# Differential attention: one VectorE operation combines the two maps of a tile, where VectorE, ScalarE and GpSimd shared it

## The chip, the cores and the metric

One core of one Trainium2 chip runs the whole program once. Its engines work side by side, each on its own list of instructions in a fixed order: TensorE (PE, with its weight loads shown apart as PEld), VectorE (DVE), ScalarE (ACT), GpSimd (POOL), and SyncE (SP), which issues most transfers. They wait for each other by semaphores. The metric is the device time of the program in microseconds (us), the median of several runs; less is better.

## What is computed

The reference is one step of a two-layer network over 1280 tokens (1024 sample tokens, 256 prompt tokens). The part that matters here is the differential attention of layer 0: eight heads, each with two attention maps, whose softmaxes are subtracted before they meet the values:

```python
s = jnp.einsum('bqhmd,bkhmd->bhmqk', qi, kf) * (DH ** -0.5)   # m = 0, 1: two maps
p = jax.nn.softmax(s, axis=-1)
a = p[:, :, 0] - lam * p[:, :, 1]
return jnp.einsum('bhqk,bkhe->bqhe', a, vf)
```

A block of 128 queries sees 1280 keys (sample queries: 1024 sample keys and 256 cached ones) or 256 keys (prompt queries). The factor `lam` is one number.

## The kernel before

`stage_b` does the attention of all eight heads. A head has ten query tiles of 128 queries, `qt` 0 to 9; tiles 0 to 7 are sample tiles with 1280 keys, tiles 8 and 9 prompt tiles with 256. So there are 64 wide tiles and 16 narrow ones. Each engine's order is the order in which the Python loop over `(h, qt)` calls the steps (`manual_schedule`); there is no planner. One round of that loop works on three tiles at once: `t`, whose scores are new, `u`, the tile before, and `p`, the tile two before (`LAG`).

The steps of a wide tile `t`:

- `scores` (L987, L988): TensorE writes the two maps' scores to PSUM, `X0` and `X1` (1024 keys each) and `Y` (the other 256 keys of both).
- `maxima` (L1003, L1005, L1007): VectorE takes the maxima, from PSUM, and joins them in a 128x1 operation `mx` (L1007) whose two inputs are both in SBUF.
- `exps` (L1013, L1014): ScalarE writes the exponentials to SBUF, `e0` and `e1` (128x1280 each, f32), with their sums. `e0` has three buffers, `e1` two.
- `ratio` (L1020 to L1025): VectorE makes `r`, per query: minus `lam` times the sum of map 0 over the sum of map 1.
- `combine` (L1031, L1033, L1034): `e0 + r * e1`, written into `e0`. The first 256 columns are one VectorE operation (L1031), called right behind `ratio`. The other 1024 are a ScalarE multiplication (L1033) and a GpSimd addition (L1034), called at the end of the round.
- `turn` (L1043, L1046, L1047): TensorE transposes `e0` in three groups (four, four and two blocks of 128) into one of two PSUM buffers `tp`; ScalarE writes the rounded part `ath`, VectorE the rest `atl`, and that subtraction frees the buffer. The groups of four come one round after the tile's scores, the group of two another round later.
- `values` (L46 to L48, `pv`): TensorE multiplies pairs of tiles with the values.

Between these steps the loop puts pieces of two projections (`fill`, L46 to L48, `acc`), the last steps of the head before (`finish`: `sq` on GpSimd L1063, `zb` on VectorE L1074, and others; `ms`, L1067, are 20 one-column products of it on TensorE), and the splitting of the next weights into a rounded part on ScalarE (L41) and a remainder on GpSimd (`wlo`, L42). At the end of a head's tile 9 (8 in the last head) stands a product for the modulation, `mp` (L84), whose result VectorE adds (L85).

Of the kernel before, what the change touches and what calls it, by code (L numbers as in the profile page):

```python
# [14 lines left out]
OP = mybir.AluOpType  # L15
# [350 lines left out]
class Weights:  # L366
# [5 lines left out]
    def next(s, key, steps=False):  # L372

        if s.gen is None:
            s.start()
        while s.step():
            pass
        w, s.gen = s.ahead, None
        assert s.rest.pop(0)[0] == key
        if s.rest and s.rest[0][1] is not None:  # L380
            s.start()
            while not steps and s.step():
                pass
        return w
# [520 lines left out]
def stage_b(c, wp):  # L905


    nc, tc, a, o = c.nc, c.tc, c.a, c.o
    c.dYb = c.dram.tile([128, HB, NT], F32, name="dYb")
    c.dYa = c.dram.tile([128, HB, NT], F32, name="dYa")  # L910
    with ExitStack() as es:
# [7 lines left out]
        v = nc.vector  # L919
        values_of, late = {}, []  # L920

        def flush():
            while late:
                late.pop(0)()

        def gate_steps(hd):
            hd.zb = ev.tile([128, NT], F32, name="zb", bufs=2)
            yield from z_steps(c, pa, hd.zb, 32 + hd.h, hd.h < HB - 1, late)

        def value_steps(h):  # L930

            x = ev.tile([128, NT], F32, name="x", tag="x")
            yield from project_steps(c, pa, c.w.next(('in', 32 + h), True), c.hhi, c.hlo,
                                     lambda p, off, n: nc.scalar.copy(x[:, off:off + n], p), late=late)
            flush()
            nc.sync.dma_start(o['new_cache_v'][h], x[:, LS:NT])
            vh = kq.tile([128, 12, 128], F32R, name="vh", bufs=2)
            vl = kq.tile([128, 12, 128], F32R, name="vl", bufs=2)
            values_of[h] = vh, vl
            raw_dma(nc, vh[:, 10:12], c.dVc[0][:, h])  # L940
            raw_dma(nc, vl[:, 10:12], c.dVc[1][:, h])
            n = 8 if h else 4
            for i in range(0, 10, n):
                w = min(n, 10 - i)
                p = (ps.tile([128, 8, 128], F32, name="vt", tag=f"X{i // 8}") if h else
                     pt.tile([128, 4, 128], F32, name="vt", tag="tp"))
                for q in range(w):
                    nc.tensor.transpose(p[:, q], x[:, (i + q) * 128:(i + q + 1) * 128], c.ident)
                nc.scalar.copy(vh[:, i:i + w], p[:, :w])
                v.tensor_sub(vl[:, i:i + w], p[:, :w], vh[:, i:i + w].bitcast(F32))  # L950
            yield

        def new_head(h):
            hd = Ctx()
            hd.h = h
            hd.s = sm.tile([128, 2, 10], F32, name="s", bufs=3)
            hd.kx = [kx.tile([128, 1280], F32R, name=f"kx{m}") for m in range(2)]
            for m in range(2):
                raw_dma(nc, hd.kx[m][:, 0:LS], c.dK[m][h][:, 0:LS])
                raw_dma(nc, hd.kx[m][:, LS:1280], c.dKc[m][:, h])  # L960
            return hd

        def prompt_keys(hd):
            hd.kp = [kq.tile([128, 256], F32R, name=f"kp{m}") for m in range(2)]
            for m in range(2):
                raw_dma(nc, hd.kp[m], c.dK[m][hd.h][:, LS:NT])

        def load_queries(h, qt):
            q = []
            for n, d in (("qh", c.dQh), ("ql", c.dQl)):  # L970
                t = kx.tile([128, 2, 128], F32R, name=n, bufs=2)
                src = d[h].rearrange("(m e) q -> e m q", m=2)[:, :, qt * 128:(qt + 1) * 128]
                for r in range(2):
                    raw_dma(nc, t[r * 64:(r + 1) * 64], src)
                q.append(t)
            return q
# [47 lines left out]
            v.reciprocal(t.r, sc[:, 1:2])  # L1024
            v.scalar_tensor_tensor(t.r, t.r, sc[:, 0:1], c.nlam, op0=OP.mult, op1=OP.mult)  # L1025

        def combine(t, half):

            e, nk = t.e, HALF if t.qt < 8 else 256
            if half == 0:  # L1030
                v.scalar_tensor_tensor(e[0][:, :nk], e[1][:, :nk], t.r, e[0][:, :nk], op0=OP.mult, op1=OP.add)  # L1031
            elif t.qt < 8:
                nc.scalar.mul(e[1][:, nk:], e[1][:, nk:], t.r)  # L1033
                nc.gpsimd.tensor_add(e[0][:, nk:], e[0][:, nk:], e[1][:, nk:])  # L1034

        def turn(t, b):

# [11 lines left out]
        def values(t):  # L1049
            qp, hd = t.qt // 2, t.hd  # L1050
            v0, v1 = values_of[hd.h]
            kts = [0, 1, 2, 3, 4, 5, 6, 7, 10, 11] if qp < 4 else [8, 9]
            pv = pa.tile([128, 256], F32, name="pv", tag="acc")
            for i, kt in enumerate(kts):
                mm3(nc, pv, v0[:, kt], v1[:, kt], t.at[:, i], t.al[:, i], i == 0, i == len(kts) - 1)
            nc.scalar.copy(hd.O[:, qp * 256:(qp + 1) * 256], pv)  # L1056
# [33 lines left out]
        with tc.manual_schedule(engines={ET.PE, ET.DVE, ET.Activation, ET.Pool}):  # L1090
            fill, fin, last = [value_steps(0)], [], None
            units = [(h, qt) for h in range(HB) for qt in range(10)]
            heads = {0: new_head(0)}
            tiles = {}

            def steps(q, n):
                while n and q:
                    if next(q[0], True):
                        q.pop(0)
                    else:  # L1100
                        n -= 1

            def new_tile(i):
                t = tiles[i] = Ctx()
                h, t.qt = units[i]
                t.hd, t.q = heads[h], load_queries(h, t.qt)

            new_tile(0)
            for i in range(len(units) + LAG):
                qt = i % 10  # L1110
                t, u, p = tiles.get(i), tiles.get(i - 1), tiles.pop(i - LAG, None)
                if t:
                    hd = t.hd
                    if qt == 0:
                        prompt_keys(hd)
                    if i + 1 < len(units):
                        new_tile(i + 1)
                    if qt == 8 and hd.h < HB - 1:
                        heads[hd.h + 1] = new_head(hd.h + 1)
                    if qt == 4:  # L1120
                        fill.append(value_steps(hd.h + 1) if hd.h + 1 < HB else gate_steps(hd))
                    if qt == 9 and hd.h + 1 < HB:
                        fill.append(gate_steps(hd))
                if t:
                    scores(t)
                if p and p.qt == 9:
                    values(p)
                    steps(fin, 1)
                if t:
                    maxima(t, 0)  # L1130
                steps(fill, PRE.get(qt, 0))
                lo = turn(p, 8) if p else lambda: None
                if t:
                    exps(t, 0)
                lo()
                if t:
                    maxima(t, 1)
                    exps(t, 1)
                steps(fin, FIN.get(qt, 0))
                c.w.step()  # L1140
                if p and p.qt % 2:
                    if p.qt < 9:
                        values(p)
                    if p.qt == 7:
                        fin.append(finish(p.hd))
                        steps(fin, 1)
                if t:
                    ratio(t)
                    combine(t, 0)
                steps(fill, FILL[qt] if i > 2 else 2)  # L1150
                if t and qt == (9 if hd.h + 1 < HB else 8):
                    c.mod[0].product(*mw, ps.tile([2, 128], F32, name="mp", tag="X1"))
                if u:
                    if u.qt == 0:
                        u.hd.O = wk.tile([128, NT], F32, name="O")
                    if u.qt % 2 == 0:
                        last = [wk.tile([128, 10, 256], F32R, name=n) for n in ("ath", "atl")]
                    u.at, u.al = last
                    turn(u, 0)()
                    turn(u, 4)()  # L1160
                flush()
                if t:
                    combine(t, 1)
                    if qt == 2:
                        mw = ev.tile([128, KC, 128], F32, name="mw", tag="zb" if hd.h + 1 < HB else "x", bufs=2 if hd.h + 1 < HB else 1)
                        mw = c.mod[0].load(16 + hd.h, mw, mwb)
            steps(fin, 100)
# [3 lines left out]
FILL = (2, 1, 0, 0, 2, 0, 2, 0, 0, 2)  # L1171
PRE = {8: 1, 9: 1}
LAG = 2
HALF = 256


def rope_tables():
# [844 lines left out]
```

## Time and profile before

| | |
|---|---|
| median of 3 runs | 2818.1 us (2816.56 to 2818.32) |
| the profiled execution | 2815.8 us, span 2814.0 us |
| granted TensorE clock, mean over the span | 0.962 |
| busy share of the span | PE 92%, PEld 80%, DVE 64%, ACT 38%, POOL 18% |
| stage with the attention | about 798 to 1500 us of the span |

The span is what the trace covers; the execution's time has 1.8 us more around it. Busy shares are averages over the whole span, and stages differ. A matmul's time in the trace overlaps that of the next one, so the share of PE says little of how much more it could do. In a row of the timeline the time of an operation overlaps that of the next by about 0.08 us on DVE and ACT, so the step from start to start is what counts there. A waiting operation on DVE that has been started shows as a longer operation, not as idle time.

### The profile page before, as it was taken

What the parts mean: (1) busy time and instruction counts of PE and PEld (TensorE: products, weight loads), DVE (VectorE), ACT (ScalarE), POOL (GpSimd) and SP (SyncE); (2) the same over time, 40 slices, a digit from 0 to 9 for tenths busy, and PEclk for the clock granted to TensorE, in tenths of its full rate; (3) what the DMA queues carried; (4) which work ended last, traced back from release to release, by engine and by line L of the source; (5) the groups of instructions that cost most, each with busy time, mean ns of one, the idle gap of its engine ahead of it and who ended that gap; (6) DMA issues with size and microseconds to landing.
All of it is one profiled execution on the core that took longest, in us unless ns stands there. A gap on an engine that the chain in (4) does not pass through costs nothing.

```text
span 2814.0 us, 40016 instructions
## 1 busy us (share of the span) xinstructions
PE 2578.0 (92%) x14905; PEld 2252.4 (80%) x14905; DVE 1812.6 (64%) x3636; ACT 1073.0 (38%) x2136; POOL 512.2 (18%) x434
## 2 busy tenths in 40 slices
PE   8989889995589999999998999978999999999998
PEld 6777777774577888878777878868999989999786
DVE  6889998997456787777876866675234435664332
ACT  3342233211156676666754221563223333222311
POOL 0000000000013232232331000005123333332321
PEclk9999999997899999999998999989999999999999
DMA  5534575455732221222217973322221136654422
GB/s 223 179 116 110 165 213 190 170 198 153 193 83 80 80 87 50 86 87 83 87 49 177 311 261 116 116 72 96 97 90 69 51 110 236 195 162 155 145 80 93
DMA packets 249130, 374.01 MB, mean 133 GB/s; under 512 B 39492, under 2 KB 172134, under 8 KB 245350
## 3 DMA queue, kind: packets, MB, share of 16 engines
q1 hardware_dynamic: 217160, 320.27, 36.0%
q10 hardware_dynamic: 31632, 50.53, 6.0%
q8 instruction: 117, 1.92, 0.3%
q14 instruction: 77, 0.63, 0.1%
q0 software_dynamic: 144, 0.66, 0.1%
HBM read 254.06 MB, written 104.73 MB: 128 GB/s over the span
## 4 chain that ended last, share of the span: by engine, by line
PE 46%; DVE 11%; ACT 5%; DMA 3%; issue 2%; POOL 1%; SPq 0%; DVEq 0%; ACTq 0%; POOLq 0%
PE pf L47 6%; PE pf L46 6%; PE pf L48 6%; PE oa L46 4%; PE oa L48 4%; PE oa L47 4%; ACT e L1013 2%; DVE mx L1003 2%; PE acc L46 2%; PE acc L48 2%; PE acc L47 2%; DVE atl L1047 2%; DMA owf<-w_out_o 1%; DVE e L1031 1%; ACT e L1014 1%
## 5 line engine op out<-in xcount | busy, mean ns | idle before, releaser
L48 PE MATMUL acc<-hhi,wlo 128*128 128x512 f32 (+1 forms) x1152 | 415.1, 362 | 30.3 <-DVE wlo L42 30.2
L46 PE MATMUL acc<-hhi,whi 128*128 128x512 f32 (+1 forms) x1152 | 418.7, 363 | 11.0 <-ACT O L1056 6.5
L47 PE MATMUL acc<-hlo,whi 128*128 128x512 f32 (+1 forms) x1152 | 415.3, 361 | 0.9 <-DVE hlo L218 0.2
L1034 POOL TENSOR_TENSOR e<-e,e 128x1024 f32<-128x1024 f32 x64 | 152.4, 2382 | 1106.8 <-DMA vh<-dVc 802.4
L48 PEld LDWEIGHTS acc<-hhi,wlo 128*128 128x128 f32 x1152 | 221.1, 192 | 67.8 <-DVE wlo L42 37.5
L46 PE MATMUL oa<-owh,oyh 128*128 128x512 f32 x640 | 254.1, 397 | 6.9 <-DVE t L1372 4.4
L46 PEld LDWEIGHTS acc<-hhi,whi 128*128 128x128 f32 x1152 | 221.1, 192 | 46.9 <-ACT O L1056 11.0
L48 PE MATMUL oa<-owh,oyl 128*128 128x512 f32 x640 | 253.2, 397 | 1.7 <-POOL oyl L42 1.7
L47 PE MATMUL oa<-owl,oyh 128*128 128x512 f32 x640 | 253.7, 396 | 0.0
L47 PEld LDWEIGHTS acc<-hlo,whi 128*128 128x128 f32 x1152 | 221.1, 192 | 34.6 <-DVE hlo L218 4.6
L1013 ACT ACTIVATE e<-X,mx 128x1024 f32<-128x1024 f32 x128 | 142.8, 1116 | 122.0 <-DVE mx L1007 118.8
L41 ACT CAST whi<-wf 128x512 fp32r<-128x512 f32 x146 | 89.7, 620 | 208.7 <-DMA wf<-w_glu 45.2
L1003 DVE TENSOR_REDUCE mx<-X 128x1 f32<-128x1024 f32 x128 | 155.2, 1212 | 18.9 <-PE X L988 18.9
L42 POOL TENSOR_TENSOR wlo<-wf,whi 128x512 fp32r<-128x512 f32 x64 | 83.7, 1308 | 416.1 <-ACT whi L41 400.5
L42 DVE TENSOR_TENSOR wlo<-fold,whi 128x512 fp32r<-128x512 f32 x94 | 84.4, 911 | 107.2 <-ACT whi L41 106.2
L46 PEld LDWEIGHTS oa<-owh,oyh 128*128 128x128 f32 x640 | 121.0, 189 | 37.2 <-ACT oyh L41 3.5
L48 PEld LDWEIGHTS oa<-owh,oyl 128*128 128x128 f32 x640 | 121.2, 189 | 30.7 <-POOL oyl L42 2.6
L47 PEld LDWEIGHTS oa<-owl,oyh 128*128 128x128 f32 x640 | 121.2, 189 | 27.8
L1046 ACT CAST ath<-atp 128x512 fp32r<-128x512 f32 (+1 forms) x208 | 99.3, 513 | 102.0 <-PE atp L1043 100.5
L46 PE MATMUL pf<-heh,whi 128*128 128x322 f32 x400 | 126.5, 320 | 10.7 <-ACT heh L1542 9.0
L1043 PE MATMUL atp<-ident,e 128*128 128x128 f32 x672 | 107.2, 287 | 21.7 <-DVE atl L1047 14.3
L47 PE MATMUL pf<-hel,whi 128*128 128x322 f32 x400 | 126.0, 315 | 0.4 <-DVE hel L1543 0.3
(448 smaller groups left out, 6745.6 us busy)
## 6 DMA issues: line engine op xcount, KB each, us to landing
wf<-w_in_e SPq DMA_DIRECT2D x96, 256.0 KB
raw<-w_fno SPq DMA_DIRECT2D x16, 1024.0 KB
mw<-w_mod SPq DMA_DIRECT2D x24, 512.0 KB
stg<-w_modT SPq DMA_DIRECT2D x24, 512.0 KB
u<-dU SPq DMA_DIRECT2D x16, 640.0 KB
dz<-z SPq DMA_DIRECT2D x8, 1280.0 KB
zc<-dz SPq DMA_DIRECT2D x16, 640.0 KB
qh<-dQh SPq DMA_DIRECT2D x160, 64.0 KB
```

The costliest lines, as they stand in the source:

```text
L41: nc.scalar.copy(hi, src)
L42: (le or nc.gpsimd).tensor_sub(lo, src, hi.bitcast(F32))
L46: nc.tensor.matmul(out, whi, xhi, start=start, stop=False)
L47: nc.tensor.matmul(out, whi, xlo, start=False, stop=False)
L48: nc.tensor.matmul(out, wlo, xhi, start=False, stop=stop)
L1003: v.tensor_reduce(t.mx[:, 0, m:m + 1], t.X[m], axis=AX.X, op=OP.max, negate=True)
L1013: nc.scalar.activation(t.e[m][:, :LS], t.X[m], AF.Exp, bias=b, accum_out=t.sums[:, 0, m:m + 1])
L1014: nc.scalar.activation(t.e[m][:, y0:y0 + 256], t.Y[:, m], AF.Exp, bias=b, accum_out=t.sums[:, 1, m:m + 1])
L1034: nc.gpsimd.tensor_add(e[0][:, nk:], e[0][:, nk:], e[1][:, nk:])
L1043: nc.tensor.transpose(p[:, i], t.e[0][:, (b + i) * 128:(b + i + 1) * 128], c.ident)
L1046: nc.scalar.copy(hi, p[:, :w])
L1047: return lambda: v.tensor_sub(t.al[:, b:b + w, o], p[:, :w], hi.bitcast(F32))
```

## The change

`combine` has no halves any more: where the 256-column VectorE operation stood it is now one VectorE operation over all 1280 columns of a wide tile. The ScalarE multiplication and the GpSimd addition, and the second call at the end of the round, are gone. Narrow tiles are as before. The arithmetic is the same: `e0 + r * e1`.

```diff
-        def combine(t, half):
-
-            e, nk = t.e, HALF if t.qt < 8 else 256
-            if half == 0:
-                v.scalar_tensor_tensor(e[0][:, :nk], e[1][:, :nk], t.r, e[0][:, :nk], op0=OP.mult, op1=OP.add)
-            elif t.qt < 8:
-                nc.scalar.mul(e[1][:, nk:], e[1][:, nk:], t.r)
-                nc.gpsimd.tensor_add(e[0][:, nk:], e[0][:, nk:], e[1][:, nk:])
+        def combine(t):
+
+            e, nk = t.e, 1280 if t.qt < 8 else 256
+            v.scalar_tensor_tensor(e[0][:, :nk], e[1][:, :nk], t.r, e[0][:, :nk], op0=OP.mult, op1=OP.add)
...
                 if t:
                     ratio(t)
-                    combine(t, 0)
+                    combine(t)
...
                 flush()
                 if t:
-                    combine(t, 1)
...
-HALF = 256
```

On VectorE, in the second tile of the first head, the rows before (numbers behind names are the program's own):

```order
L1025 SCALAR_TENSOR_TENSOR r<-r,s,nlam 128x1
L1031 SCALAR_TENSOR_TENSOR e_6789<-e_6790,r,e_6789 128x256
L1047 TENSOR_TENSOR atl<-atp,ath 128x4x128 x2
L1003 TENSOR_REDUCE mx<-X_6877 128x1
L1005 TENSOR_REDUCE mx<-Y 128x2
```

and the same place now:

```order
L1025 SCALAR_TENSOR_TENSOR r<-r,s,nlam 128x1
L1030 SCALAR_TENSOR_TENSOR e_6787<-e_6788,r,e_6787 128x1280
L1043 TENSOR_TENSOR atl<-atp,ath 128x4x128 x2
L1003 TENSOR_REDUCE mx<-X_6873 128x1
L1005 TENSOR_REDUCE mx<-Y 128x2
```

Nothing has moved on VectorE; one row is five times as wide, and line numbers behind it are lower by four (L1031 is now L1030, L1047 now L1043).

On GpSimd, from the first head's first wide tile to its last, the rows before:

```order
L1034 TENSOR_TENSOR e_6721<-e_6721,e_6722 128x1024
L1034 TENSOR_TENSOR e_6789<-e_6789,e_6790 128x1024
L42 TENSOR_TENSOR wlo<-wf,whi 128x512
L1034 TENSOR_TENSOR e_6875<-e_6875,e_6876 128x1024
L42 TENSOR_TENSOR wlo<-wf,whi 128x512
L1034 TENSOR_TENSOR e_6994<-e_6994,e_6995 128x1024
L1034 TENSOR_TENSOR e_7090<-e_7090,e_7091 128x1024
L1034 TENSOR_TENSOR e_7177<-e_7177,e_7178 128x1024
L42 TENSOR_TENSOR wlo<-wf,whi 128x512
L1034 TENSOR_TENSOR e_7273<-e_7273,e_7274 128x1024
L42 TENSOR_TENSOR wlo<-wf,whi 128x512
L1034 TENSOR_TENSOR e_7365<-e_7365,e_7366 128x1024
```

and now, in the same stretch and on to the second head:

```order
L42 TENSOR_TENSOR wlo<-wf,whi 128x512 x4
L1059 TENSOR_TENSOR sq<-O 128x1024
L1059 TENSOR_TENSOR sq<-O 128x256
L42 TENSOR_TENSOR wlo<-wf,whi 128x512 x4
L1059 TENSOR_TENSOR sq<-O 128x1024
```

The 64 additions have gone; the weight splits and the squares stay in their order.

## Rows read from the trace of the kernel before

**Rows 1.** Stages: length, busy PE, PEld, DVE, ACT, POOL (instructions), clock, DMA, GB/s.

```profile
798.00:1500.00 702.00, 653.27 (x4047) 561.91 (x4045) 519.27 (x1034) 445.96 (x985) 210.87 (x110) 0.98 0.25 76
1064.12:1152.03 87.91, 83.84 (x516) 72.74 (x515) 65.66 (x133) 55.69 (x123) 26.65 (x14) 0.96 0.26 78
```

**Rows 2.** Waits, 798 to 1500 us: waiting engine and line, releaser; total, times, longest.

```profile
ACT e L1013 <- DVE mx L1007: 118.8, 63, 2.7
...
DVE mwb L85 <- PE mp L84: 56.1, 7, 8.0
...
PEld atp L1043 <- DVE atl L1047: 26.8, 30, 3.9
...
PEld atp L1043 <- POOL e L1034: 8.7, 7, 1.5
```

**Rows 3.** Timeline of VectorE, one wide tile: start, length, line, operation, [idle before].

```profile
1098.35 1.22 DVE L1003 TENSOR_REDUCE mx<-X 128x1 f32<-128x1024 f32 x1
...
1100.20 0.63 DVE L1007 TENSOR_TENSOR mx<-mx 128x1 f32<-128x1 f32 x1
1100.75 0.41 DVE L1047 TENSOR_TENSOR atl<-atp,ath 128x256 fp32r<-128x256 f32 x1
...
1105.26 0.48 DVE L1031 SCALAR_TENSOR_TENSOR e<-e,r,e 128x256 f32<-128x256 f32 x1
1105.67 1.28 DVE L1047 TENSOR_TENSOR atl<-atp,ath 128x512 fp32r<-128x512 f32 x2
1106.87 1.21 DVE L1003 TENSOR_REDUCE mx<-X 128x1 f32<-128x1024 f32 x1
```

**Rows 4.** Timeline of GpSimd, same tile.

```profile
1098.42 2.39 POOL L1034 TENSOR_TENSOR e<-e,e 128x1024 f32<-128x1024 f32 x1 [6.12 <-PE atp L1043]
```

**Rows 5.** Groups by line and shape: count, busy us, mean ns, idle before.

```profile
L1034 POOL TENSOR_TENSOR e<-e,e 128x1024 f32<-128x1024 f32 x64 | 152.4, 2382 | 1106.8 <-DMA vh<-dVc 802.4 <-issue 185.0 <-PE X L988 44.3
...
L1033 ACT ACTIVATE e<-e,r 128x1024 f32<-128x1024 f32 x64 | 75.3, 1177 | 0.3 <-DVE r L1025 0.3
...
L1031 DVE SCALAR_TENSOR_TENSOR e<-e,r,e 128x256 f32<-128x256 f32 x80 | 67.3, 841 | 7.6 <-DVE r L1025 0.5
...
L1007 DVE TENSOR_TENSOR mx<-mx 128x1 f32<-128x1 f32 x128 | 47.5, 371 | 4.4
```

**Rows 6.** Lines L1031, L1007, L1074: least, median and greatest ns; first and last start.

```profile
L1031 DVE SCALAR_TENSOR_TENSOR e<-e,r,e x80: 483/485/1481, 802.4 to 1498.3; 128x256 f32<-128x256 f32 x80
...
L1007 DVE TENSOR_TENSOR mx<-mx x128: 159/160/1444, 794.5 to 1485.1; 128x1 f32<-128x1 f32 x128
...
L1074 DVE SCALAR_TENSOR_TENSOR zb<-zb,subg,O x8: 1542/1546/1547, 917.6 to 1506.9; 128x1280 f32<-128x1280 f32 x8
```

**Rows 7.** Timeline of VectorE around a combination beside a weight split.

```profile
1087.99 1.46 DVE L1031 SCALAR_TENSOR_TENSOR e<-e,r,e 128x256 f32<-128x256 f32 x1
1089.37 1.28 DVE L1047 TENSOR_TENSOR atl<-atp,ath 128x512 fp32r<-128x512 f32 x2
```

**Rows 8.** Timeline of GpSimd, same place.

```profile
1087.89 1.28 POOL L42 TENSOR_TENSOR wlo<-wf,whi 128x512 fp32r<-128x512 f32 x1 [4.38 <-ACT whi L41]
```

**Rows 9.** Timeline of VectorE: idle time behind the combination, in a first tile.

```profile
1070.19 0.48 DVE L1031 SCALAR_TENSOR_TENSOR e<-e,r,e 128x256 f32<-128x256 f32 x1
1071.00 0.42 DVE L1047 TENSOR_TENSOR atl<-atp,ath 128x256 fp32r<-128x256 f32 x1 [0.33 <-ACT ath L1046]
1071.51 0.69 DVE L901 SCALAR_TENSOR_TENSOR zb<-zb,acc 128x512 f32<-128x512 f32 x1
```

**Rows 10.** Timeline of TensorE, products in tile 2, then tile 3's scores.

```profile
1082.02 3.25 PE L1067 MATMUL ms<-ones,sq 128*128 128x1 f32 x20 [0.49 <-DVE zb L901]
...
1088.16 0.63 PE L988 MATMUL X<-kx,ql 128*128 128x512 f32 x1
...
1090.24 0.39 PE L987 MATMUL X<-kx,qh 128*128 128x512 f32 x1
```

**Rows 11.** The stretch of those scores, columns as in rows 1.

```profile
1086.70:1090.30 3.60, 3.60 (x13) 3.07 (x12) 2.86 (x6) 3.13 (x8) 1.67 (x2) 0.52 0.02 7
```

## The prediction

> **What bounds the kernel now.** I read the windows first, then the waits of the attention stage, then the timelines of one head. The stage lasts 702 us of the 2814.0 us span; TensorE shows 653 us of it busy, its weight loads 562 us (80%), VectorE 519 us (74%), ScalarE 446, GpSimd 211 [rows 1]. A head takes 87.9 us. No engine is full, so the question is which chain sets the step from tile to tile.
>
> In a wide tile VectorE takes the maxima, ScalarE then writes the exponentials, VectorE combines, subtracts `atl`, and starts on the next tile's maxima. In the tile shown this ring takes 8.52 us, from L1003 at 1098.35 to L1003 at 1106.87 [rows 3]. Both neighbours wait for VectorE: ScalarE for the joined maxima, 63 times, 118.8 us; TensorE's weight loads for the transposes 30 times, 26.8 us, for `atl`, whose subtraction frees the transposes' buffer [rows 2]. So in most wide tiles the ring through VectorE and ScalarE is the bound and TensorE follows. At the end of a head it is the other way: VectorE sits idle 8.0 us each time until TensorE has the product `mp` [rows 2]. A delay of VectorE in the tiles before is not made up there, because TensorE's own work of that stretch stands behind those tiles' transposes in its list.
>
> **What the change adds.** One VectorE operation grows from 256 to 1280 columns, 64 times. The same instruction form with a pointer scalar and two SBUF inputs stands elsewhere in this stage at 1280 columns: L1074, median 1546 ns; at 256 columns L1031 has 485 [rows 6]. The difference is 1.061 us, and 64 x 1.061 = **+67.9 us**. L1074 lies between 1542 and 1547 ns and the undisturbed L1031 between 483 and 485 [rows 6], so the bounds are close: 67.6 to 68.1. The growth stands between `ratio` and `atl`, inside the ring; queued behind it are the two `atl` subtractions and the next maxima, and for these TensorE and ScalarE wait.
>
> **What it removes.** 75.3 us on ScalarE and 152.4 us on GpSimd [rows 5]. Taken alone this is worth nothing: ScalarE's next work is the exponentials, for which it waits anyway, and GpSimd's sum is read a round later. It is worth something in three places.
>
> First, the pair. L1007 joins two 128x1 values and takes 159 or 160 ns in at least half of its 128 cases, but 371 on average and 1444 at most [rows 5, 6]. In the tile shown it took 0.63 us, starting at 1100.20; the GpSimd addition ran from 1098.42 to 1100.81, and L1007 ended with it [rows 3, 4]. The large reductions from PSUM beside it kept their length. So an operation with both inputs in SBUF waits for GpSimd's to end. With the additions gone this falls away: 128 x (371 - 160) ns = **-27.0 us**, all of it in front of the exponentials. It can't be more from L1007; it can be nothing if another GpSimd operation takes the place.
>
> The Trainium skill has this rule (SBUF - State Buffer, Who interferes with whom): a VectorE instruction with two SBUF inputs and a GpSimd instruction that reads SBUF exclude each other for the whole instruction, whoever starts first. The trace agrees, 0.63 us in place of 0.16. By a rule without exclusion the relief would be nothing and the sum 27 us higher.
>
> L1031 shows the same wait, 841 ns on average over 80 against a median of 485, 28.5 us in all [rows 5, 6]. But these are the weight splits: L42 started at 1087.89, L1031 at 1087.99 and took 1.46 [rows 7, 8]. The splits stay, both follow the same exponentials on ScalarE, so I leave this wait as it is: 0, with a gain of 28.5 as its bound (a rival below).
>
> Second, the first tile of a head. There VectorE waits 0.33 us behind L1031 for a cast of ScalarE that follows TensorE. From L1031 to L1047 is 0.81 us where the other tile has 0.41, and from L1047 to L901 0.51 where L1047 alone needs 0.34 [rows 3, 9]. That hides 0.40 + 0.17 = 0.57 us of the growth, in seven heads (the first has no head before it): **-4.0 us**; bounds 0 and 4.6.
>
> Third, the last wide tile of a head. There TensorE waits for the GpSimd sum 7 times, 8.7 us, 1.24 us each [rows 2]. This goes. But what TensorE does next are the scores of tile 9, which wait for the exponentials of tile 8, and these now come behind a longer chain on VectorE. Following the tile's steps I get 0.8 of the 1.24 us back: **-5.6 us** in seven heads, bounds 0 and 8.7.
>
> **The sum.** 67.9 - 27.0 - 4.0 - 5.6 = **+31.3 us**. The profiled execution took 2815.8 us, 1.8 more than its span; with 31.3 it is 2847.1. It lies 2.3 under the median of the runs, 2818.1, which would become 2849.4. I give 2848.
>
> Of the rest: transfers keep their number. The exponentials into an old buffer of `e1` waited for GpSimd and now wait for a combination two tiles back, long done. VectorE's busy time in the stage becomes 519 + 68 - 27 = 560 of 733 us, 76%.
>
> **The rivals.**
>
> *TensorE covers it; faster.* TensorE's busy share of the stage is 93%, its weight loads' 80%, more than VectorE's [rows 1]. If TensorE were the bound, the growth would lie in VectorE's 26% of idle time, and what counts is the one removed wait that TensorE had: 8.7 us for GpSimd's sum [rows 2], which gives 2807 to 2809. It decides if TensorE's 30 waits for `atl` are not in the ring but leftovers of its own lateness. Against it stand those 30 waits, and 87.9 us a head where the work of a head repeats with TensorE kept waiting. A page of the Trainium skill leads this way (Perfetto Trace Analysis, Identifying the Most-Contended Engine): judge TensorE by its weight loads' busy share and work on the engine with the highest occupancy. By that rule TensorE with 80% bounds the stage and 76% on VectorE costs nothing; the trace has the 80%, but its waits point to VectorE.
>
> *The order at the pair flips; no change.* In the shown place GpSimd's split is 0.10 us ahead of L1031 [rows 7, 8]. If the split now came behind, L1031 would no longer wait, and GpSimd would, for weights that are needed later. All 28.5 us would be saved: 31.3 - 28.5 = +2.8, so 2819 to 2821. For it: 0.1 us is little. Against it: both starts hang on the same exponentials, and neither is moved against the other. The Trainium skill's page named above speaks for the wait at whichever comes second; with the shown order that stays VectorE.
>
> *No relief; slower still.* If L1007 keeps its wait and the two covers fail, the whole 67.9 us is added: 2884 to 2886. Against it: L1007's long cases end with the additions.
>
> *The clock falls more often; slower.* Around 1086.70 to 1090.30 the granted clock was 0.52 on average, so largely at the lower of its two levels, 1.2 in place of 2.4 GHz; before it TensorE had waited and done one-column products for 3.25 us. A 512-column matmul showed 0.63 us there and 0.39 right behind, and such a stretch lasted some 3.6 us [rows 10, 11]. The ring's growth makes TensorE wait 1 to 2 us more in front of the transposes of tiles 3 to 6. One more such stretch a head, with half of its 3.6 us on the path, costs 1.8 x 8 = 14 us: 2863. For it: the stage's mean is 0.98 [rows 1], it can fall. Against it: TensorE's lateness is partly hidden when VectorE is the bound.
>
> **How the numbers follow.** The forecast with its 31 us has 0.66, the clock 0.14, TensorE's cover 0.08, the flip 0.07, no relief 0.05. The forecast's own bounds: 67.6 - 27.0 - 4.6 - 8.7 = 27.3 with all of each relief, so 2843 on the execution's time, and 68.1 - 20 = 48 with three quarters of the first relief and no cover, so 2866 on the median. From 2828 (half of the L1031 waits gone as well, 14 us under the lower bound) to 2866 the range holds the forecast and the clock, 0.80. Faster or slower is counted from 0.2%, 5.6 us, about what a measurement of this kernel can tell from no change. Faster has the 0.08 of the cover. The flip's 0.07 is no change, and 0.02 more from small sums. Slower has the rest, 0.83.
>
> **What would show it.** In the changed kernel's profile: the new combination near 1.55 us at its median, with some 30 cases 0.9 us longer; L1007 near 0.16 us on average; ScalarE's wait for the maxima shorter for each tile, but its idle time before the exponentials not; a head of about 92 us in place of 87.9, with the growth in tiles 1 to 7; TensorE's waits for `atl` up by some 20 us and its wait for GpSimd's sum gone; the other stages as they were. The prediction is wrong if heads keep 87.9 us, if long L1007 remain, or if the combination takes other than 1.5 to 1.6 us when nothing blocks it.

## The result and the profile after

The changed kernel takes 2843.05 us (median of 4 runs, 2842.29 to 2844.82) against 2817.33 us before, measured beside it: 25.7 us more, a ratio of 1.010 with a 95% interval of 1.0086 to 1.0113. The profiled execution took 2842.29 us with a span of 2840.4.

Where the time went is read from the windows, first over the stage and then over one head (columns as in [rows 1]):

```profile
798.00:1527.00 729.00, 667.75 (x4038) 567.43 (x4037) 561.06 (x1037) 377.49 (x918) 59.61 (x47) 0.96 0.25 73
...
1072.28:1164.13 91.85, 85.32 (x516) 72.58 (x515) 71.08 (x133) 47.40 (x115) 7.64 (x6) 0.96 0.25 75
```

A head takes 91.85 us where it took 87.91 [rows 1]. From the first L1003 of the stage (792.6 us before, 789.8 after) to the end of the last `atl` (1501.3 and 1527.0) it is 708.7 us before and 737.1 after: 28.5 us more. What follows the stage is as it was (1312.7 and 1313.4 us). The stage's start differs by 2.8 us between the two executions, but over the profiled executions of this study, whose programs agree up to there, it lies between 786.9 and 794.7, so this is no effect of the change.

The groups of VectorE, with the two lines that answer to L1031 and L1007 of [rows 5], and the least, median and greatest length of the combination:

```profile
L1030 DVE SCALAR_TENSOR_TENSOR e<-e,r,e 128x1280 f32<-128x1280 f32 x64 | 129.1, 2018 | 2.3
...
L1007 DVE TENSOR_TENSOR mx<-mx 128x1 f32<-128x1 f32 x128 | 21.9, 171 | 4.4
```

```profile
L1030 DVE SCALAR_TENSOR_TENSOR e<-e,r,e x80: 483/1552/2586, 799.6 to 1523.9; 128x1280 f32<-128x1280 f32 x64, 128x256 f32<-128x256 f32 x16
```

The undisturbed combination is 1552 ns, and its mean of 2018 says that many are longer; L1007 fell from 371 to 171 ns. The same tile as in [rows 3], tile 4 of the fourth head, on VectorE:

```profile
1109.30 1.21 DVE L1003 TENSOR_REDUCE mx<-X 128x1 f32<-128x1024 f32 x1
...
1111.14 0.16 DVE L1007 TENSOR_TENSOR mx<-mx 128x1 f32<-128x1 f32 x1
1111.22 0.42 DVE L1043 TENSOR_TENSOR atl<-atp,ath 128x256 fp32r<-128x256 f32 x1
...
1115.39 0.22 DVE L1025 SCALAR_TENSOR_TENSOR r<-r,s,nlam 128x1 f32<-128x1 f32 x1
1115.65 1.55 DVE L1030 SCALAR_TENSOR_TENSOR e<-e,r,e 128x1280 f32<-128x1280 f32 x1
1117.12 1.28 DVE L1043 TENSOR_TENSOR atl<-atp,ath 128x512 fp32r<-128x512 f32 x2
1118.31 1.22 DVE L1003 TENSOR_REDUCE mx<-X 128x1 f32<-128x1024 f32 x1
```

From maxima to maxima it is 9.01 us where it was 8.52. From the combination to `atl` it is 1.47 in place of 0.41; from L1007 to the next operation 0.08 in place of 0.55. The difference of the two, 0.59, is nearly the tile's growth of 0.49; most of what is left is idle time in front of the combination, which is taken up below.

Beside a weight split (tile 2), on VectorE and then on GpSimd, as in [rows 7, 8]:

```profile
1096.88 2.52 DVE L1030 SCALAR_TENSOR_TENSOR e<-e,r,e 128x1280 f32<-128x1280 f32 x1
1099.33 1.27 DVE L1043 TENSOR_TENSOR atl<-atp,ath 128x512 fp32r<-128x512 f32 x2
```

```profile
1096.78 1.27 POOL L42 TENSOR_TENSOR wlo<-wf,whi 128x512 fp32r<-128x512 f32 x1 [8.74 <-ACT whi L41]
```

The split still starts 0.10 us ahead, and the combination still waits for its end.

The waits of the stage:

```profile
ACT e L1013 <- DVE mx L1007: 107.3, 63, 3.8
...
DVE mwb L85 <- PE mp L84: 56.9, 7, 8.1
PEld atp L1039 <- DVE atl L1043: 56.5, 66, 3.4
```

TensorE's weight loads wait for `atl` 56.5 us where it was 26.8 [rows 2], and no wait for GpSimd's sum is left. At the end of a head VectorE waits for the product as before.

### The profile page after: what moved, and what is told of

It reads as the page before. It is cut to its first block, busy times and chain, and to the rows that moved or that the text cites. A ratio compares the mean times of both kernels' runs of the same rounds, so it can differ in the third digit from the quotient of the medians.

```text
span 2840.4 us, 39703 instructions
## 1 busy us (share of the span) xinstructions
PE 2597.2 (91%) x14905; PEld 2263.3 (80%) x14905; DVE 1854.8 (65%) x3636; ACT 1006.4 (35%) x2072; POOL 359.6 (13%) x370
## 5 line engine op out<-in xcount | busy, mean ns | idle before, releaser
L1003 DVE TENSOR_REDUCE mx<-X 128x1 f32<-128x1024 f32 x128 | 155.3, 1214 | 19.8 <-PE X L988 19.8
L1030 DVE SCALAR_TENSOR_TENSOR e<-e,r,e 128x1280 f32<-128x1280 f32 (+1 forms) x80 | 136.9, 1711 | 2.8
L1039 PEld LDWEIGHTS atp<-ident,e 128*128 128x128 f32 x672 | 80.6, 149 | 63.5 <-DVE atl L1043 56.5
```

The source lines that it names most:

```text
L1003: v.tensor_reduce(t.mx[:, 0, m:m + 1], t.X[m], axis=AX.X, op=OP.max, negate=True)
L1039: nc.tensor.transpose(p[:, i], t.e[0][:, (b + i) * 128:(b + i + 1) * 128], c.ident)
```

## The experiments

Each was timed in turn with the kernel before on the same chip. The table has the medians; the base of each call is beside it. That base differs by 2 us from call to call, so a difference between kernels of different calls is no surer than that.

| kernel | us | before, same call | ratio (95%) |
|---|---|---|---|
| e1_removal_alone | 2787.46 | 2815.7 | 0.9901 (0.9886 to 0.9917) |
| e2_growth_alone | 2854.57 | 2815.7 | 1.0138 (1.0123 to 1.0153) |
| f1_split_later | 2812.96 | 2815.7 | 0.999 (0.998 to 0.9999) |
| f2_half_512 | 2801.74 | 2815.7 | 0.995 (0.9933 to 0.9967) |
| g1_one_input_join | 2794.14 | 2816.08 | 0.9928 (0.9913 to 0.9943) |
| g4_join_and_split | 2774.12 | 2816.08 | 0.9854 (0.9838 to 0.9869) |
| g7_none_on_vector | 2787.56 | 2816.08 | 0.9899 (0.9882 to 0.9915) |
| g6_half_512 | 2783.72 | 2817.73 | 0.9879 (0.9865 to 0.9894) |
| g4_again | 2770.62 | 2817.73 | 0.9835 (0.9817 to 0.9852) |

**The removal by itself.** The kernel before, without the second half of `combine`:

```diff
-            elif t.qt < 8:
-                nc.scalar.mul(e[1][:, nk:], e[1][:, nk:], t.r)
-                nc.gpsimd.tensor_add(e[0][:, nk:], e[0][:, nk:], e[1][:, nk:])
```

Expected: 

> The kernel before, with the ScalarE multiplication and the GpSimd addition left out and nothing put in their place, so that 1024 of a wide tile's 1280 columns keep map 0 alone. It has the removal without the growth. Theory of the pair (the ring through VectorE and ScalarE bounds most tiles, and L1007 waited for GpSimd's addition): L1007 falls to about 171 ns on average, 25 us go, and with TensorE's wait for GpSimd's sum (5 to 9 us) and some 0.06 us less in front of each combination (4 us) the time is 2779 to 2787 us. Rival, TensorE bounds and only its own wait counts: 2808 to 2812 us.

It took 2787.46 us, 28.2 less than before. The groups show L1007 without any wait:

```profile
L1007 DVE TENSOR_TENSOR mx<-mx 128x1 f32<-128x1 f32 x128 | 20.4, 159 | 4.4
```

ScalarE's and GpSimd's shares, then, were not free work beside the ring: together they cost it 28 us. The time is 0.5 us above the range that the pair gave and 20 us under the rival's.

**The growth by itself.** The changed kernel, with work of the removed kind back on columns that nobody reads:

```diff
+                    if qt < 8:
+                        nc.scalar.mul(t.e[1][:, 256:], t.e[1][:, 256:], t.r)
+                        nc.gpsimd.tensor_add(t.e[1][:, 256:], t.e[1][:, 256:], t.e[1][:, 256:])
```

Expected: 

> The changed kernel, with a ScalarE multiplication and a GpSimd addition of the old sizes put back on columns of e1 that nobody reads any more. It has VectorE's growth without the removal. Theory of the pair: long L1007 come back, about 25 us in all, and the time is 2862 to 2872 us, near the 68 us that the growth costs without relief less what the covers hide. Rival, the removal gave nothing and the growth costs less than its length: 2843 us as the changed kernel.

It took 2854.57 us, 11.5 more than the changed kernel: the direction of the theory, 7 us under its range. The groups of GpSimd and VectorE tell why the size was missed:

```profile
L1161 POOL TENSOR_TENSOR e<-e 128x1024 f32<-128x1024 f32 x64 | 121.1, 1893 | 1183.7 <-DMA qh<-dQh 802.3 <-ACT e L1160 370.2 <-DMA wf<-w_in_e 8.2
...
L1007 DVE TENSOR_TENSOR mx<-mx 128x1 f32<-128x1 f32 x128 | 32.0, 250 | 4.4
```

My addition read one array twice and took 1893 ns, not the 2382 of the one that it stood for [rows 5], so it ended sooner and held L1007 up for less: 250 ns on average, 128 x (250 - 171) = 10.1 us more than in the changed kernel. The time rose by about that. The run is also less than the whole removal undone: nobody reads the new sum, so neither TensorE's wait for it nor the idle time in front of the combination (2.9 us, as in the changed kernel) came back.

**Which operand waits.** The kernel before with L1007 in another form:

```diff
-                v.tensor_tensor(b, t.mx[:, 0, m:m + 1], b, op=OP.min)
+                v.tensor_scalar(b, t.mx[:, 0, m:m + 1], b, None, op0=OP.min)
```

Expected: 

> The kernel before, with L1007's join written as a tensor_scalar: one of its two 128x1 inputs is read as a pointer scalar, the work of GpSimd and ScalarE stays. Theory of the pair (VectorE waits for GpSimd only where two streams come from SBUF): L1007 falls to about 160 ns though the GpSimd addition runs beside it, and about 25 us go: 2789 to 2795 us. Rival, any VectorE operation on SBUF that starts inside GpSimd's waits: L1007 stays at 371 ns on average and the time at 2813 to 2818 us.

It took 2794.14 us, 21.9 less than before, though GpSimd's addition is as it was (2383 ns). A tile of it on VectorE, then GpSimd at the same place:

```profile
1093.53 0.21 DVE L1007 TENSOR_SCALAR mx<-mx 128x1 f32<-128x1 f32 x1
```

```profile
1091.75 2.40 POOL L1034 TENSOR_TENSOR e<-e,e 128x1024 f32<-128x1024 f32 x1 [6.24 <-ACT e L1033]
```

The join runs inside the addition, which goes on to 1094.15, and takes 0.21 us; over all 128 its mean is 214 ns. So what waited in L1007 was not access to SBUF as such but a second streamed input from SBUF. Nothing else in the program was changed, and L1031, which has a pointer scalar and two streams, does wait [rows 7, 8]. This is the other half of the rule in the Trainium skill (SBUF - State Buffer, Who interferes with whom): with at most one SBUF input, and outside the modes in which it uses both of its ports, VectorE does not contend with GpSimd. The trace agrees, 214 ns, if the pointer scalar isn't counted as such an input.

**The wait that stayed.** The changed kernel with the weight split called elsewhere:

```diff
                 steps(fin, FIN.get(qt, 0))
-                c.w.step()
...
                 flush()
+                c.w.step()
                 if t:
```

Expected: 

> The changed kernel, with the step that splits the next weights called behind the transposes of the round instead of in front of the combination. Theory: L42 on GpSimd then runs beside the subtractions and the reductions from PSUM, which don't wait for it, and ends before the next L1007; the 64 combinations lose their 29.8 us of waiting, and the time is 2813 to 2820 us. Rival, the wait only moves to another operation (L1007, or TensorE waiting for weights that come later): 2838 to 2845 us.

It took 2812.96 us, at the lower edge of its range, 30.1 less than the changed kernel and level with the kernel before. L1007's mean stays at 171 ns, so the wait did not move there, and the combination of a wide tile is 1552 ns everywhere:

```profile
L1030 DVE SCALAR_TENSOR_TENSOR e<-e,r,e x80: 483/1552/1554, 799.5 to 1494.0; 128x1280 f32<-128x1280 f32 x64, 128x256 f32<-128x256 f32 x16
```

and where the two meet it is GpSimd that waits, in the timeline of tile 1, VectorE and then GpSimd:

```profile
1074.19 1.55 DVE L1030 SCALAR_TENSOR_TENSOR e<-e,r,e 128x1280 f32<-128x1280 f32 x1
```

```profile
1075.35 1.54 POOL L42 TENSOR_TENSOR wlo<-wf,whi 128x512 fp32r<-128x512 f32 x1 [5.11 <-ACT whi L41]
```

The split starts inside the combination and takes 1.54 us, not 1.28. So the pair goes to whoever starts first, in both directions, and here the loser has time.

**A size between.** The kernel before with `HALF = 512`. Expected: 

> The kernel before with 512 columns of a wide tile on VectorE and 768 on ScalarE and GpSimd. VectorE's part grows by 64 x 0.267 = 17 us; ScalarE's gets about 0.3 and GpSimd's 0.6 us shorter, so GpSimd ends 0.9 us earlier in the round, which is as much as the long L1007 were long (0.5 to 0.9 us a tile). Theory of the pair: 20 to 25 us of waiting go, and the time is 2808 to 2815 us. Rival, VectorE's columns alone count: 2833 to 2836 us.

It took 2801.74 us, 14.0 less than before and 6 under the range. GpSimd's addition is 1830 ns, and L1007 is long (over 175 ns) in 16 cases where it was in 42:

```profile
L1034 POOL TENSOR_TENSOR e<-e,e 128x768 f32<-128x768 f32 x64 | 117.1, 1830 | 1112.6 <-DMA vl<-dVc 801.5 <-issue 177.9 <-PE X L987 65.3
...
L1007 DVE TENSOR_TENSOR mx<-mx 128x1 f32<-128x1 f32 x128 | 23.6, 184 | 4.4
```

L1007 gives back 128 x (371 - 184) = 23.9 us for a growth of 17. Those alone make -7, and the stage is 10.2 us shorter in the traces; the rest I haven't taken apart (covers such as those in the prediction, and TensorE's wait for the sum, which fell from 8.7 to 5.5 us).

**Both waits away.** g1's form of L1007, and the split moved as in f1, in the kernel before. Expected: 

> g1_one_input_join, and the step that splits the next weights called behind the transposes of the round, in front of the second half of the combination. Theory: both waits at the pair go, 25 us of L1007 and 28 us of L1031, and the time is 2760 to 2775 us, a little more if TensorE becomes the bound. Rival, GpSimd's addition now comes 1.3 us later, behind the split, and holds something else up (L1031 or TensorE's transposes): 2780 to 2795 us.

It took 2774.12 us. Run again beside the next kernel, expected: 

> g4_join_and_split once more on the same chip as g6_half_512, as its base: 2770 to 2778 us by any theory.

It took 2770.62 us. This is the fastest version found, 1.5 to 1.7% under the kernel before. L1031 is now at its 484 ns:

```profile
L1031 DVE SCALAR_TENSOR_TENSOR e<-e,r,e 128x256 f32<-128x256 f32 x80 | 38.8, 484 | 7.2
...
L1007 DVE TENSOR_SCALAR mx<-mx 128x1 f32<-128x1 f32 x128 | 27.4, 214 | 4.5
```

**How much belongs on VectorE, once nothing waits at the pair.** g4_join_and_split with 512 columns on VectorE. Expected: 

> g4_join_and_split with 512 columns on VectorE and 768 on ScalarE and GpSimd: what the growth costs where no wait at the pair is left. If VectorE's length alone counts, 64 x 0.267 = 17 us more than g4_join_and_split, 2789 to 2793 us; if TensorE's 10 us of waits for GpSimd's sum matter as much, and covers hide some, 2770 to 2782 us.

2783.72 us, 13.1 more than g4_again for 17 us more on VectorE. Three quarters of the length show in the time. It fell between the two ranges, some 4 us under what length alone gives even when that is reckoned from 2770.6. TensorE's wait for GpSimd's sum fell by 4.9 us (10.4 in g4_again, 5.5 here), which is near to that; that it is the cause was not tested. And with none (`HALF = 0`, the VectorE operation of wide tiles left out):

Expected: 

> g4_join_and_split with all 1280 columns of a wide tile on ScalarE and GpSimd and none on VectorE, the other end from the changed kernel. Theory (VectorE's length in the ring counts): 64 x 0.47 = 30 us less on VectorE, of which the covers hide some: 10 to 25 us under g4_join_and_split. Rival, TensorE is the bound once the waits are gone, or GpSimd's longer addition (near 3 us) comes too late for the transposes: no faster than g4_join_and_split, or slower.

2787.56 us, 13.4 more than g4_join_and_split. Here the rival held. The addition takes 2939 ns, and the waits show who is late, in g4_join_and_split and then here:

```profile
PEld atp L1043 <- POOL e L1034: 10.4, 14, 1.0
```

```profile
L1036 POOL TENSOR_TENSOR e<-e,e 128x1280 f32<-128x1280 f32 x64 | 188.1, 2939 | 961.2 <-DMA vl<-dVc 803.5 <-issue 71.9 <-ACT e L1035 42.1
...
PEld atp L1045 <- POOL e L1036: 22.3, 15, 2.0
```

TensorE's weight loads wait 22.3 us for GpSimd's sum in place of 10.4. So, with the pair's waits away, the best width has two sides, and of the three tried (0, 256, 512) it is the old 256.

## Why the prediction was right, step by step

**The bound.** The ring through VectorE and ScalarE was said to set the step of the wide tiles, and TensorE the end of a head. Tile by tile (six middle heads, from start to start of the maxima) the change added 0.40, 0.38, 1.00, 0.99, 0.51, 0.44, 0.59 and 0.28 us in tiles 0 to 7, and took 0.61 and 0.19 back in tiles 8 and 9. That is growth in the tiles where VectorE leads, and none at the end. g1_one_input_join tested it from the other side: taking time from VectorE alone shortens the kernel. e1_removal_alone agrees, but it took work from ScalarE and GpSimd too.

**The terms.** In us over the stage, as forecast and as the two traces give it. The idle time in front of the combination has a row of its own, and the rows of a head's first tile and of its end are without it:

| term | forecast | measured |
|---|---|---|
| growth of the combination, 64 x | +67.9 | +68.3 (1552 - 485 ns) |
| L1007 no longer waits | -27.0 | -25.6 (47.5 to 21.9) |
| the combination's own waits for splits | 0 | +1.3 (28.5 to 29.8) |
| hidden in the first tile, seven heads | -4.0 | -4.2 (0.59 of 1.07 hidden) |
| end of a head, TensorE's wait for GpSimd, seven heads | -5.6 | -4.6 (0.65 a head) |
| idle time in front of the combination | none | -4.7 (7.6 to 2.3 + 0.6) |
| tile 4 of the last head | none | -1.0 (hidden behind the wait in which ScalarE waits for weights) |

The measured column sums to +29.5, and the stage grew by 28.5. The missing 1.0 is the sum of smaller differences of either sign, such as 1.3 us more in tiles 2 and 3 of the first head and 1.2 us less in tile 8 of the last. What L1007 keeps, 128 x (171 - 159) ns or 1.5 us in all, lies in tile 1 of a head, beside GpSimd's square `sq`. The two large terms were right to about 5%, the two covers to 1 us. The forecast of 31.3 was 5.6 above the 25.7 of the timed runs and inside their interval (0.0086 to 0.0113 of 2817 is 24.2 to 31.8). The forecast's own lower bound, +27.3, was too high for 25.7, though not for the 28.5 of the stage; it lacked the idle time below. Of the signs named, TensorE's waits for `atl` rose by 29.7 us where some 20 were named; the combination came as named, with 30 of its 64 wide cases 0.99 us longer than the median.

**What was missed.** Idle time in front of the combination was not in the sum. Before, from L1025 to L1031 it is 0.26 us in tiles 1 and 2, whose buffer of `e0` last held a narrow tile, and 0.32 in the others, whose buffer GpSimd wrote three tiles earlier; after, it is 0.26 there too (1115.39 to 1115.65 in the tile above). Before, the combination waited for two semaphores in those tiles, one of them GpSimd's, with a semaphore instruction of its own in VectorE's queue (63 in the trace); after, for one, and that instruction is gone. The row in front of L1031 of [rows 3], and the instruction, before:

```profile
1104.93 0.22 DVE L1025 SCALAR_TENSOR_TENSOR r<-r,s,nlam 128x1 f32<-128x1 f32 x1
```

```profile
L1031 DVEq EVENT_SEMAPHORE  x63: 21/21/21, 831.7 to 1498.2; - x63
```

That it is the instruction, and not the wait itself, that costs the 0.07 us was not tested apart. In e1_removal_alone, where GpSimd's semaphore is gone too, the idle time is 2.8 us:

```profile
L1031 DVE SCALAR_TENSOR_TENSOR e<-e,r,e 128x256 f32<-128x256 f32 x80 | 68.8, 859 | 2.8
```

**The rivals.** TensorE's cover fell with the result: its 80% of weight loads was more than VectorE's 74%, and yet VectorE's growth showed: within a head the two take turns, as the tiles above show. The flip did not happen by the change, since the split stayed 0.10 us ahead; f1_split_later brought it about and returned 30 us, where the rival had put 28.5 on it. No relief: L1007's fall excludes it. The clock: its granted mean (1.00 is the upper of its two levels, 2.4 GHz) did fall, over the stage from 0.98 to 0.96, and in the six middle heads from 0.96 to 1.00 before to 0.94 to 0.98 after. But a head's length did not follow it. The second and third heads, before and then after:

```profile
887.55:975.86 88.31, 81.56 (x516) 69.62 (x515) 65.79 (x133) 55.67 (x123) 26.67 (x14) 1.00 0.26 78
975.86:1064.12 88.26, 83.91 (x516) 72.85 (x515) 65.71 (x133) 55.67 (x123) 26.66 (x14) 0.96 0.26 78
```

```profile
888.60:980.45 91.85, 83.81 (x516) 70.47 (x515) 71.08 (x134) 47.34 (x115) 7.65 (x6) 0.98 0.26 76
980.45:1072.28 91.83, 86.31 (x516) 73.91 (x515) 71.07 (x134) 47.44 (x115) 7.64 (x6) 0.94 0.25 75
```

At 1.00 and 0.96 they took 88.31 and 88.26 us, at 0.98 and 0.94 91.85 and 91.83. So the rival's condition came in part, and its price did not.

## What to carry to other kernels

Before work is moved onto or off an engine, look at the lengths of that engine's small operations: a 128x1 operation that takes 0.16 us at the median and 0.37 on average is waiting, and the trace shows it as busy. In these traces a VectorE operation with two streams from SBUF and a GpSimd operation that reads SBUF beside it take turns, so work that GpSimd does "for free" is paid for by the next such operation in VectorE's list; another form of that operation, or another place for GpSimd's, can be worth more than moving the work. Here the change exchanged 68 us in the ring for 40 us of relief and covers, while one operand's form and one moved call took 42 to 47 us off the kernel before.

## What the runs showed of the hardware that was not expected

- A 128x1 minimum with one input read as a pointer scalar takes 214 ns in all of g1_one_input_join (212 to 217), beside GpSimd's additions or not; with both inputs streamed it takes 159 alone and up to 1444 ns beside them [rows 6].
- A GpSimd addition of 128x1024 f32 takes 1893 ns when both inputs are one array and 2382 when they are two.
- A GpSimd subtraction that starts 0.39 us ahead of the end of a VectorE combination takes 1.54 us in place of 1.28 (f1_split_later, tile 1 above): the exclusion works both ways.
